# A hybrid attention/mLSTM diffusion layer: attention of all token blocks ahead of the FFN, and the FFN in one pass over split float16 weights

## The chip, the cores and the metric

One core of one Trainium2 chip runs the program. The metric is the device time of one execution in microseconds; the kernel before takes 1610.73 us (median of 3 runs, 1610.1 to 1613.63). The profile shows PE (TensorE; weight loads apart as PEld), DVE (VectorE), ACT (ScalarE), POOL (GpSimd) and the DMA queues, most of which SP issues.

## The reference

One layer over 9 blocks of 128 tokens: block 0 is a prompt that reads itself alone, blocks 1 to 8 are latent tokens that read all latent keys and a cache (9 x 128 keys). All in float32.

```python
h = rmsnorm(x, norm1_w) * (1 + sc1) + sh1
aq, ak, av, mq, mk, mv, mo, mg = split(h @ w_in)            # w_in 1024 x 2832
attn_o = attention(rope(rmsnorm(aq)), keys, vals)           # 8 query heads, 2 key heads, width 64
hm = rmsnorm(mlstm_bidir(mq, mk, mv, gates)) * sigmoid(mo)  # 4 heads, both directions
x  = x + g1 * (concat([attn_o, hm]) @ w_out)                # w_out 1024 x 1024
h2 = rmsnorm(x, norm2_w) * (1 + sc2) + sh2
g, u = split(h2 @ w_gu)                                     # w_gu 1024 x 5632
x  = x + g2 * ((silu(g) * u) @ w_down)                      # w_down 2816 x 1024
y  = rmsnorm(x, final_norm_w)
```

## The kernel before

float32 products are kept by splitting each operand into a high and a low part and adding three products (high by high, high by low, low by high). The input projection and the values product use float16 pairs scaled by powers of two. The output projection and the FFN use pairs of the type fp32r: `load_piece` (L138) loads a weight piece of 512 KB, rounds it on ACT (L151, `whi`) and subtracts on POOL or, every third, on DVE (L134, `wlo`).

**Stages.** Modulation vectors, norm and input projection; four mLSTM heads (`head_project`, `head_mlstm`); then attention, output projection, norm and FFN. These last are done for *chunks* of three blocks (CB = 3, 384 tokens). `GROUPS` and `LAST` (L37, L38) cut the 22 slices of 128 FFN columns (f) into five groups. For each chunk and group, `gate_up` (L1337) makes two products per f with 24 matmuls of 384 columns each (`products`, L1333 to L1335), then tanh on ACT (L1360), two DVE operations (L1361, L1362) and the split of the result into `hl` (L1365 on ACT, L134 on POOL); `down` (L1369) multiplies by w_down with 512-column matmuls (L1152 to L1154) into float32 rows `x1` by `add_gated` (L1138: multiply L1141, add L1142). So all of w_gu and w_down is loaded and split three times, once per chunk.

**Attention.** `attention(c, ...)` (L973) is a generator over the heads of a chunk. A head of a latent block has six 384-column matmuls into the PSUM tile `S` (L1075; one buffer of three banks, so the next head's `S` waits for the exponential), a maximum on DVE (L1077), an exponential on ACT (L1078), two one-column DVE operations (L1079, L1080), the high part of the weights on ACT (L1081), the low part on DVE (L1082), and two DMA transposes that SP issues (L1083, L1084). Two heads later the values product takes 18 matmuls of 256 columns per pair of heads (L999), with ACT (L1001, `ol`) and DVE (L1003, `oT`) behind it. `psum["mm"]` holds four more banks, taken by `bank()`.

**Order.** A scheduler places instructions by priority and its own estimate of time, engine by engine; each engine then runs its list in order. The program order that it starts from is set by hand. Chunk 0's attention (16 heads and the prompt) stands beside the rest of the query projection, `prefill` (L1189, the mLSTM half of the output projection for all blocks) and the first two FFN slices (`gate_up_pair`). Attention of chunks 1 and 2 is woven by `weave` (L62, L1491) into the FFN of the chunk ahead, about one unit of attention for every seven FFN products, and the attention half of the output projection (`attn_out`, L1240) and the second norm (`norm2`, L1285) follow inside that FFN. The last group of the last chunk is `down_last` (L1396), which ends with the final norm block by block.

Of the kernel before, what the change touches and what calls it, by code (L numbers as in the profile page):

```python
# [39 lines left out]
NG = 4  # L40
# [5 lines left out]
def hybrid_step(ctx: ExitStack, tc: tile.TileContext, I: dict, O: dict):  # L46
# [52 lines left out]
    psum = {"mm": ctx.enter_context(tc.tile_pool(name="pB", bufs=4, space=PSUM, reuse_waits="tile"))}  # L99
# [7 lines left out]
    x1_d = [drp.tile([P, D], F32, name=f"x1_d{i}") for i in range(CB)]  # L107
# [50 lines left out]
    def powers(v, n):  # L158

        v = v[0:n]  # L160
        dve.tensor_scalar(out=v[:, 0:1], in0=v[:, 0:1], scalar1=2.0 ** -16, scalar2=None, op0=ALU.max)
# [70 lines left out]
    vsc = cp.tile([P, 4], F32, name="vsc")  # L232

# [14 lines left out]
    one1 = gp.tile([1, P], F32, name="one1")  # L248
    hsc = gp.tile([P, 4], F32, name="hsc")
    hs2 = gp.tile([P, 1], F32, name="hs2")  # L250
    dve.memset(one1, 1.0)

# [126 lines left out]
    dve.memset(G, 0.0)  # L379

# [55 lines left out]
    def ada_rest(adp):  # L436


        def rows_of(n, j, q, half):
            a4 = adp.tile([P, 4, 256], F32, name=nm("a4"), tag="a4", bufs=3)  # L440
# [53 lines left out]
    def evac_kvg(b, ps):  # L494
# [3 lines left out]
        for t in range(2):  # L498
            g4, b4 = (v.rearrange("p (d t h) -> p d t h", d=2, t=2)[:, :, t] for v in (ps[:, 256:272], gbias))
            dve.scalar_tensor_tensor(out=Gv[:, :, t, 4 * b : 4 * b + 4], in0=g4, scalar=kvg.inv, in1=b4, op0=ALU.mult, op1=ALU.add)  # L500

# [261 lines left out]
    def head_mlstm(h, st):  # L763
# [3 lines left out]
        q1 = QT[:, 1, :].rearrange("p (d x) -> p d x", d=2)  # L767
        wvs = {}

        def weighted(b):  # L770
            if b not in wvs:
                wv = wvs[b] = mlp.tile([P, 2, P + 1], F32, name=nm("wv"), tag="wv", bufs=NB)
                dve.tensor_tensor(out=wv, in0=bc(blocks[b][2], 1, [P, 2, P + 1]), in1=bc(q1[:, :, 4 * b + h], 2, [P, 2, P + 1]), op=ALU.mult)
            return wvs[b]
# [9 lines left out]
        weighted(0)  # L784
        for d in range(2):
            weighted(seqs[d][1])
        yield
        for j in range(NBL):
            for d in range(2):
                b = seqs[d][j]  # L790
                pc = bank()
                mm(pc[:, 0 : P + 1], blocks[b][1], wvs[b][:, d], start=True, stop=True)
                if j + 2 < NBL:
                    weighted(seqs[d][j + 2])
# [128 lines left out]
    kwork = k_work(qp, cc, ss, kw)  # L923
    scan = head_mlstm(2, sts[2])
    weave(head_project(3, sts[3]), beside((scan, 1.15), (kwork, 0.5)), 56, 56)
# [8 lines left out]
    mix_spare = [t[:, 2 * (NB + 1) * P :].rearrange("p (k x) -> p k x", k=4) for t in big]  # L934
# [631 lines left out]
```

## Time and profile before

| | |
|---|---|
| median of 3 runs | 1610.73 us |
| the profiled execution | 1617.88 us, span 1616.1 us |
| PE busy | 1521.3 us (94%), 8688 matmul records |
| PEld, DVE, ACT, POOL busy | 1260.8, 940.1, 730.2, 615.8 us |
| mean granted TensorE clock | 0.968 |
| DMA | 227.98 MB, mean 141 GB/s |

A matmul's busy time is its latency, and matmuls overlap; what one adds to PE is the distance from its start to the next one's. Rows of a timeline are: start, duration, engine, line, operation, tiles, shape, count, and in brackets how long the engine was idle before it and who ended that. A windows row is: stretch, length, then busy time and count of PE, PEld, DVE, ACT and POOL, the granted clock, the DMA share and GB/s.

### The profile page before, as it was taken

How to read it: one execution, taken by the hardware profiler on the slowest of the kernel's cores; microseconds unless marked ns; L12 is line 12 of the kernel's file. 1: busy time of each engine (PE TensorE's matmuls, PEld its weight loads, DVE VectorE, ACT ScalarE, POOL GpSimd, SP SyncE). 2: the span in 40 equal slices, each digit the busy share in tenths (PEclk: the TensorE clock that was granted, in tenths of full speed). 3: DMA queues.
4: the chain of work that ended last, by engine and by line, in shares of the span. 5: the costliest groups of instructions: out<-in, count | busy, mean ns of one | idle time of the engine just before them, and what ended most of it. 6: DMA issues, size and time to landing. Idle time of an engine off the chain costs nothing. (4 is left out here: it accounts for less than half of the span.)

```text
span 1616.1 us, 23209 instructions
## 1 busy us (share of the span) xinstructions
PE 1521.3 (94%) x8688; PEld 1260.8 (78%) x8688; DVE 940.1 (58%) x1821; ACT 730.2 (45%) x1240; POOL 615.8 (38%) x376
## 2 busy tenths in 40 slices
PE   5899999899788868999999999999999999999996
PEld 2655665576557758988999999898898989999995
DVE  3944353947787565677753547767764474332445
ACT  3744343435454455655532344565552443333322
POOL 0411020503247453433345344443344445544443
PEclk8899999999899987999999999999999999999998
DMA  9445353211165664787843546787774445534441
GB/s 344 132 131 144 102 134 73 84 19 32 41 171 119 147 159 100 166 194 169 190 146 118 156 144 208 189 180 165 169 178 124 142 134 174 156 122 147 143 130 66
DMA packets 383270, 227.98 MB, mean 141 GB/s; under 512 B 169174, under 2 KB 345766, under 8 KB 383158
## 3 DMA queue, kind: packets, MB, share of 16 engines
q1 hardware_dynamic: 382598, 225.68, 52.9%
q8 instruction: 68, 1.11, 0.3%
q10 hardware_dynamic: 560, 0.83, 0.1%
q14 instruction: 44, 0.36, 0.1%
HBM read 178.80 MB, written 9.33 MB: 116 GB/s over the span
## 5 line engine op out<-in xcount | busy, mean ns | idle before, releaser
L134 POOL TENSOR_TENSOR wlo<-raw,whi 128x1024 fp32r<-128x1024 f32 x146 | 357.8, 2454 | 450.3 <-ACT whi L151 416.4
L151 ACT CAST whi<-raw 128x1024 fp32r<-128x1024 f32 x219 | 224.3, 1025 | 372.0 <-DMA raw<-in_w_gu_dram 127.8
L1334 PE MATMUL mm<-aTl,whi 128*128 128x384 f32 (+2 forms) x1088 | 366.8, 337 | 0.0
L1335 PE MATMUL mm<-aTh,wlo 128*128 128x384 f32 (+2 forms) x1088 | 366.4, 337 | 0.0
L1333 PE MATMUL mm<-aTh,whi 128*128 128x384 f32 (+2 forms) x1088 | 365.1, 337 | 0.9 <-DVE tn L1361 0.9
L1333 PEld LDWEIGHTS mm<-aTh,whi 128*128 128x128 f32 x1088 | 206.9, 190 | 2.1 <-DVE tn L1361 1.5
L1334 PEld LDWEIGHTS mm<-aTl,whi 128*128 128x128 f32 x1088 | 206.9, 190 | 1.0 <-POOL aTl L134 0.3
L1335 PEld LDWEIGHTS mm<-aTh,wlo 128*128 128x128 f32 x1088 | 207.0, 190 | 0.1
L134 DVE TENSOR_TENSOR wlo<-raw,whi 128x1024 fp32r<-128x1024 f32 (+1 forms) x73 | 88.2, 1208 | 132.9 <-ACT whi L151 132.7
L1152 PE MATMUL mm<-whi,hl 128*128 128x512 f32 x372 | 147.0, 398 | 1.0 <-ACT hl L1365 0.9
L1153 PE MATMUL mm<-wlo,hl 128*128 128x512 f32 x372 | 147.2, 397 | 0.0
L1154 PE MATMUL mm<-whi,hl 128*128 128x512 f32 x372 | 144.4, 397 | 0.7 <-POOL hl L134 0.7
L1082 DVE SCALAR_TENSOR_TENSOR pl<-pr,st,ph 128x1152 f16<-128x1152 f32 x64 | 109.5, 1711 | 46.7 <-ACT ph L1081 46.6
L487 PE MATMUL wi<-ipair,hT 128*128 128x384 f16 (+2 forms) x384 | 124.9, 326 | 2.8 <-ACT ipair L215 2.8
L488 PE MATMUL wi<-ipair,hT 128*128 128x384 f16 (+2 forms) x384 | 124.9, 325 | 0.0
L489 PE MATMUL wi<-ipair,hT 128*128 128x384 f16 (+2 forms) x384 | 124.4, 325 | 0.3 <-POOL hT L134 0.3
L1361 DVE SCALAR_TENSOR_TENSOR tn<-tn,mm 128x384 f32<-128x384 f32 (+2 forms) x68 | 36.7, 540 | 144.4 <-PE mm L1335 110.0
L134 POOL TENSOR_TENSOR hl<-tn,hl 128x384 fp32r<-128x384 f32 x66 | 81.9, 1241 | 96.5 <-ACT hl L1365 90.4
L1142 DVE TENSOR_TENSOR x<-x,t 128x512 f32<-128x512 f32 x102 | 116.1, 1158 | 0.8
L1078 ACT ACTIVATE pr<-S,st 128x1152 f32<-128x1152 f32 x64 | 78.3, 1223 | 80.4 <-DVE st L1077 77.6
L1141 DVE TENSOR_TENSOR t<-mm,gl 128x512 f32<-128x512 f32 x106 | 70.8, 683 | 40.6 <-PE mm L1154 15.8
L1077 DVE TENSOR_REDUCE st<-S 128x1 f32<-128x1152 f32 x64 | 86.5, 1351 | 13.2 <-PE S L1075 12.8
(370 smaller groups left out, 2678.0 us busy)
## 6 DMA issues: line engine op xcount, KB each, us to landing
raw<-in_w_gu_dram SPq DMA_DIRECT2D x132, 512.0 KB
raw<-in_w_down_dram SPq DMA_DIRECT2D x60, 512.0 KB
a<-in_w_ada_dram SPq DMA_DIRECT2D x32, 512.0 KB
gl<-g_d SPq DMA_DIRECT2D x36, 256.0 KB
aw<-in_w_ada_dram SPq DMA_DIRECT2D x16, 512.0 KB
iraw<-in_w_in_dram SPq DMA_DIRECT2D x32, 256.0 KB
raw<-in_w_out_dram SPq DMA_DIRECT2D x15, 512.0 KB
x<-in_x_sample_dram SPq DMA_DIRECT2D x13, 512.0 KB
```

Of the source, the lines that this page charges most:

```text
L134: (dve if eng == "dve" else pool).tensor_tensor(out=out, in0=full, in1=hi, op=ALU.subtract)
L151: nc.scalar.copy(hi[:, :n], raw[:, :n])
L487: mm(ps[:, :n], ah, wh[:, k % 2, c0 : c0 + n], start=(k == 0), stop=False)
L488: mm(ps[:, :n], ah, wl[:, k % 2, c0 : c0 + n], start=False, stop=False)
L489: mm(ps[:, :n], al, wh[:, k % 2, c0 : c0 + n], start=False, stop=(k == KD - 1))
L1142: eng.tensor_tensor(out=x1[:, cs], in0=x1[:, cs], in1=t, op=ALU.add)
L1152: mm(ps, ah, wh[:, k % 2, :], start=(k == 0), stop=False)
L1153: mm(ps, ah, wl[:, k % 2, :], start=False, stop=False)
L1154: mm(ps, al, wh[:, k % 2, :], start=False, stop=(k == nk - 1))
L1333: mm(ps, wh[:, k, :], th[:, k, :], start=(k == 0), stop=False)
L1334: mm(ps, wh[:, k, :], tl[:, k, :], start=False, stop=False)
L1335: mm(ps, wl[:, k, :], th[:, k, :], start=False, stop=(k == KD - 1))
```

## The change

Attention, `prefill`, the attention half of the output projection (`out_rest`) and `norm2` run for all nine blocks before the FFN. `FILL` is the amount of other matmul work, in us by the writer's unit costs, that the program order puts beside one head. x1 and the normed h2 of all blocks stay in SBUF, h2 as float16 pairs scaled by one power of two (`bound_h2`). The FFN then makes one pass: four groups of 6, 6, 6 and 4 slices; each w_gu piece is loaded once, measured (ACT, sum of squares), scaled and split into float16 (`Piece`); w_down is split once into float16 pairs and written to a DRAM tensor `wd_d` (`split_down`), from which `down9` loads ready pairs, three times in all. A group's results wait as float32 (`tn`), and `rescale` makes float16 pairs of them under one scale for the group while the next group's products run. At the end of attention its PSUM tiles are released and the FFN gets eight banks. No POOL work is left in the FFN. The mLSTM scan's weighting is done per direction, and some tiles move between pools.

```diff
-GROUPS = [(0, 4), (4, 4), (8, 4), (12, 5), (17, 5)]
-LAST = [(0, 5), (5, 5), (10, 4), (14, 4), (18, 4)]
+GROUPS = [(0, 6), (6, 6), (12, 6), (18, 4)]
+SLOTS = 24
+FILL = 2.2
...
+    def out_rest():
+        ws = out_pieces(0)
+        for b in range(NB):
+            while b not in done:
                 yield False
...
+            for n in range(2):
                 ps = out_block(ws, n, th, tl)
+                add_gated(x1[b], ps, gx[n] if b == 0 else gs[n], n, pool)
+                yield 2.8
+            if b > 0:
+                yield from norm2(b - 1)
+            rs[b] = stats(x1[b : b + 1])[0]
+            yield 0.1
...
+    fill = chain(prefill(), out_rest())
+    for v in att:
+        due = min(due + v, 5.0)
+        while due > 0.0:
+            u = next(fill, None)
+            if not u:
+                break
+            due -= u
+    emit(fill)
...
+    pieces[0].load()
+    pieces[0].measure()
+    pieces[0].scales()
+    pieces[0].convert()
+    es_at.close()
+    es_p.close()
+    es_b.close()
+    bp = ctx.enter_context(tc.tile_pool(name="bp", bufs=1, reuse_waits="tile"))
+    psum["mm"] = ctx.enter_context(tc.tile_pool(name="p8", bufs=8, space=PSUM, reuse_waits="tile"))
...
+    def gate_up9(g):
...
+                products(ps[:, 0:CT], wh, wl, h2[c][:, 0], h2[c][:, 1])
...
+            tn = bp.tile([P, CT], F32, name=nm("tn"), tag="hl", bufs=SLOTS)
+            act(tn, pg[:, 0:CT], AF.Tanh, scale=p.v[:, 6:7])
+            dve.scalar_tensor_tensor(out=tn, in0=tn, scalar=1.0, in1=pu[:, 0:CT], op0=ALU.add, op1=ALU.mult)
+            dve.scalar_tensor_tensor(out=tn, in0=tn, scalar=p.v[:, 7:8], in1=pg[:, 0:CT], op0=ALU.mult, op1=ALU.mult)
+            act(jk[:, 0:CT], tn, AF.Abs, accum_out=g["st"][:, i : i + 1])
...
+    def down9(g):
+        for c in range(NCH):
+            for n in range(2):
+                banks = [bank() for _ in range(CB)]
+                for j in range(0, g["nf"], 2):
+                    w = down_piece(g, j, n)
+                    for i, ps in enumerate(banks):
+                        down_products(ps, g, j, b, w)
```

**Where instructions move.** First PE during the attention of chunk 1. Before (S is a head's scores, `mm` with `aTh`/`aTl` the FFN's gate and up product, `po` the values product):

```order
L1333 MATMUL mm_10156<-aTh_9420,whi_10159 128x384
L1334 MATMUL mm_10156<-aTl_9421,whi_10159 128x384
L1335 MATMUL mm_10156<-aTh_9420,wlo_10160 128x384
L1333 MATMUL mm_10156<-aTh_9420,whi_10159 128x384
L1334 MATMUL mm_10156<-aTl_9421,whi_10159 128x384
L1075 MATMUL S_10135<-kst_4226,qT_9905 128x384 x6
L999 LDWEIGHTS vs
L999 MATMUL po_10189<-phT_9996,vs 128x256
L1335 MATMUL mm_10156<-aTh_9420,wlo_10160 128x384
L1333 MATMUL mm_10156<-aTh_9420,whi_10159 128x384
```

In the changed kernel, late in attention:

```order
L1029 LDWEIGHTS vs
L1029 MATMUL po_7528<-plT_7308,vs 128x256
L1103 MATMUL S_7465<-kst_4270,qT_7084 128x384 x6
L1103 MATMUL S_7557<-kst_4271,qT_7084 128x384 x6
L1103 MATMUL S_7602<-kst_4271,qT_7084 128x384 x6
L1029 LDWEIGHTS vs
L1029 MATMUL po_7622<-phT_7423,vs 128x256
L1029 LDWEIGHTS vs
L1029 MATMUL po_7622<-plT_7424,vs 128x256
```

Before, FFN matmuls stand on both sides of a head's scores; now the scores of three heads follow each other with nothing between.

Next DVE at the same place. Before (one head; t and x are `add_gated`):

```order
L1077 TENSOR_REDUCE st_11429<-S_11430 128x1
L1141 TENSOR_TENSOR t_2146_11303<-mm_11269,gl_11255 128x512
L1079 RECIPROCAL st_11429<-st_11429 128x1
L1142 TENSOR_TENSOR x_1020_5218<-x_1020_5218,t_2146_11303 128x512
L1080 TENSOR_SCALAR st_11429<-st_11429 128x1
L1141 TENSOR_TENSOR t_2154_11351<-mm_11306,gl_11255 128x512
L1141 TENSOR_TENSOR t_2155_11354<-mm_11307,gl_11255 128x512
L1142 TENSOR_TENSOR x_1020_5218<-x_1020_5218,t_2154_11351 128x512
L1142 TENSOR_TENSOR x_1020_5218<-x_1020_5218,t_2155_11354 128x512
L1082 SCALAR_TENSOR_TENSOR pl_11428<-pr_11426,st_11429,ph_11427 128x1152
```

In the changed kernel (three heads):

```order
L1105 TENSOR_REDUCE st_7650<-S_7651 128x1
L1110 SCALAR_TENSOR_TENSOR pl_7600<-pr_7598,st_7601,ph_7599 128x1152
L1107 RECIPROCAL st_7650<-st_7650 128x1
L1108 TENSOR_SCALAR st_7650<-st_7650 128x1
L1105 TENSOR_REDUCE st_7729<-S_7730 128x1
L1110 SCALAR_TENSOR_TENSOR pl_7649<-pr_7647,st_7650,ph_7648 128x1152
L1107 RECIPROCAL st_7729<-st_7729 128x1
L1108 TENSOR_SCALAR st_7729<-st_7729 128x1
L1110 SCALAR_TENSOR_TENSOR pl_7728<-pr_7726,st_7729,ph_7727 128x1152
L1033 SCALAR_TENSOR_TENSOR oT_7527<-po_7761,vsc,ol_7780 64x128 x2
L1105 TENSOR_REDUCE st_7789<-S_7790 128x1
```

The FFN's operations are gone from between a head's; the low part `pl` of a head stands behind the next head's maximum in the first two and ahead of it in the third.

Last, PE where attention ends. Before, chunk 2's output projection (`mx`) runs straight into FFN products that were ready:

```order
L1184 MATMUL mm_12270<-whi_12180,mx_12251 128x512
L1185 MATMUL mm_12270<-wlo_12181,mx_12251 128x512
L1186 MATMUL mm_12270<-whi_12180,mx_12251 128x512
L1333 MATMUL mm_12309<-aTh_9420,whi_12312 128x384
L1334 MATMUL mm_12309<-aTl_9421,whi_12312 128x384
L1335 MATMUL mm_12309<-aTh_9420,wlo_12313 128x384
```

In the changed kernel:

```order
L1183 MATMUL mm_8285<-wlo_6822,kst_4270 128x512
L1184 MATMUL mm_8285<-whi_6821,kst_4271 128x512
L1362 MATMUL mm_8356<-fv_8351,ones 128x2
L1285 LDWEIGHTS wpair_8366
L1285 MATMUL mm_8400<-h_1399_7094,wpair_8366 128x384
L1286 LDWEIGHTS wpair_8366
L1286 MATMUL mm_8400<-h_1399_7094,wpair_8366 128x384
```

Behind the last output block stands the 2-column matmul that measures the first FFN weight piece (L1362), and only behind it the first FFN product, whose weights (`wpair`) are converted by that measure.

More of the change, by code (lines that the diff above doesn't have):

```diff
@@ L1160, in out_pieces @@
-    def out_pieces(half, own=None):
+    def out_pieces(half):
         ws = []
@@ L1166, in out_pieces @@
                 rows = w_out[r0 : r0 + 2 * P, n * 512 : (n + 1) * 512].rearrange("(a p) n -> p a n", p=P)
[L1167 to L1168 removed]
+                pieces.append(load_piece([(full_view, rows)], (2, 512), 1))
             ws.append(pieces)
         return ws
[L1172 to L1178 removed]
     def out_block(ws, n, th, tl):
@@ L1277, in stats @@
+            yield 0.1
     def stats(rows):
@@ new lines, in hybrid_step @@
+    pieces = [Piece(0, lambda: wp.tile([P, 1024], F32, name=nm("braw"), tag="raw", bufs=2), ("whi", "wlo"))]
+    pieces += [Piece(f) for f in range(1, NF)]
+    pieces[0].load()
[7 more added lines that the diff above has]
+    psum["mm"] = ctx.enter_context(tc.tile_pool(name="p8", bufs=8, space=PSUM, reuse_waits="tile"))
+    pieces[1].load()
```

716 lines of the change are left out of this document (370 added, 346 removed).

## The prediction

> **What bounds the kernel now.** I read the busy time by stage first, because the share over the whole span (PE 94%) is a mean over unlike stages.
>
> ```profile
> span 1616.1 us, 23209 instructions
> PEclk8899999999899987999999999999999999999998
> 0.00:445.00 445.00, 398.80 (x2614) 253.73 (x2615) 253.22 (x779) 199.52 (x521) 92.20 (x107) 0.94 0.40 112
> 445.00:600.00 155.00, 134.88 (x664) 102.00 (x662) 111.22 (x189) 78.57 (x107) 85.61 (x52) 0.92 0.67 155
> 600.00:650.00 50.00, 39.73 (x231) 36.66 (x230) 24.45 (x55) 25.96 (x44) 16.56 (x10) 0.80 0.41 90
> 650.00:1616.00 966.00, 947.92 (x5185) 868.39 (x5183) 551.17 (x801) 426.19 (x570) 421.47 (x207) 1.00 0.58 155
> ```
>
> The reader is to see four stages. Up to 445 us nothing of weight is changed. From 445 to 650 us, chunk 0's attention, PE is idle for about 30 us and its clock falls to 0.92 and 0.80. From 650 us, the FFN with the attention of chunks 1 and 2 inside, PE is idle for 18 of 966 us at full clock: PE bounds this stage, and DVE (57%), ACT and POOL have room. So the weights split three times cost nothing there; the FFN's price is its matmuls, and attention's long DVE and ACT chain is covered by them.
>
> The price of a matmul is the distance between starts. From timelines of PE, the first and last row of four unbroken runs (40, 12, 29 and 33 rows of one shape):
>
> ```profile
> 843.10 0.34 PE L1335 MATMUL mm<-aTh,wlo 128*128 128x384 f32 x1
> 849.86 0.34 PE L1335 MATMUL mm<-aTh,wlo 128*128 128x384 f32 x1
> 169.49 0.33 PE L487 MATMUL wi<-ipair,hT 128*128 128x384 f16 x1
> 171.28 0.33 PE L489 MATMUL wi<-ipair,hT 128*128 128x384 f16 x1
> 515.60 0.40 PE L1185 MATMUL mm<-wlo,aTh 128*128 128x512 f32 x1
> 522.14 0.39 PE L1186 MATMUL mm<-whi,aTl 128*128 128x512 f32 x1
> 443.21 0.39 PE L487 MATMUL mm<-ipair,hT 128*128 128x512 f16 x1
> 450.13 0.38 PE L489 MATMUL mm<-ipair,hT 128*128 128x512 f16 x1
> ```
>
> That is 6.76/39 = 0.173 us for fp32r of 384 columns, 1.79/11 = 0.163 for float16 of 384, 6.54/28 = 0.234 for fp32r of 512, 6.92/32 = 0.216 for float16 of 512.
>
> **The FFN.** By the code it has 22 x 2 x 3 x 24 = 3168 products of 384 columns and 22 x 9 x 2 x 3 = 1188 of 512, before and after. By the pitches they take 3168 x 0.173 + 1188 x 0.234 = 826 us before and 516 + 257 = 773 us after: 53 us saved. This is the whole gain on PE. Removed besides are two thirds of the w_gu loads and splits, and all POOL work; these lay beside PE and are worth nothing by themselves. New work beside PE: per slice f and three chunks, DVE has six operations on `tn`, two piece splits, one w_down split and three pair splits; even at the 1.4 us that a 1152-column operation takes below, the four large ones and nine small ones stay under 15 us, against 144 x 0.163 + 54 x 0.216 = 35 us of PE. The round trip of w_down pairs through DRAM has over 100 us before the first group needs it, and each 512 KB piece then serves 18 matmuls (3.9 us), five buffers deep. I cost both at nothing; uncovered they would cost a few us at a group's start. For the group scales and the first pieces' waits I add 5: the FFN takes 778 us.
>
> The Trainium skill ("TensorE: Matmul & The Clock Gate", section "Back-to-back issue gap") gives about 131 ns as the sustained spacing of 512-column matmuls beside an isolated 216; this trace's unbroken run has 0.216. By 131 ns the 1188 matmuls would take 101 us less than by the row; the row stands.
>
> **Attention now stands almost alone.** What it costs is the loop of one head, since S has one buffer: scores on PE, maximum on DVE, exponential on ACT, next scores. Timelines of two places of chunk 0, a filled one (522) and one where PE had nothing else (574 to 589):
>
> ```profile
> 522.36 1.21 PE L1075 MATMUL S<-kst,qT 128*128 128x384 f32 x6
> 523.61 1.36 DVE L1077 TENSOR_REDUCE st<-S 128x1 f32<-128x1152 f32 x1 [0.29 <-PE S L1075]
> 525.01 1.22 ACT L1078 ACTIVATE pr<-S,st 128x1152 f32<-128x1152 f32 x1 [0.37 <-DVE st L1077]
> 526.24 0.28 PE L999 MATMUL po<-plT,vs 128*128 128x256 f16 x1 [2.12 <-DMA plT<-pl]
> ...
> 574.65 1.34 DVE L1077 TENSOR_REDUCE st<-S 128x1 f32<-128x1152 f32 x1
> 576.27 1.21 ACT L1078 ACTIVATE pr<-S,st 128x1152 f32<-128x1152 f32 x1
> 577.63 2.29 PE L1075 MATMUL S<-kst,qT 128*128 128x384 f32 x6 [1.19 <-ACT pr L1078]
> 579.95 0.42 PE L999 MATMUL po<-phT,vs 128*128 128x256 f16 x1
> 579.96 1.36 DVE L1077 TENSOR_REDUCE st<-S 128x1 f32<-128x1152 f32 x1 [0.90 <-PE S L1075]
> 583.15 0.35 PE L999 MATMUL po<-plT,vs 128*128 128x256 f16 x1
> 588.32 1.35 DVE L1077 TENSOR_REDUCE st<-S 128x1 f32<-128x1152 f32 x1
> ```
>
> At full clock a loop is 1.25 (scores to maximum) + 1.40 + 1.22 + 0.15 (exponential's end at 577.48 to the next scores at 577.63) = 4.0 us. Where PE has idled, the same six score matmuls take 2.29 instead of 1.21, and sixteen values matmuls from 579.95 to 583.15 stand 0.213 us apart: the clock is halved and the loop is 5.1. The interval measured there, 574.65 to 579.96, is 5.3. The rows of the other operations:
>
> ```profile
> L1077 DVE TENSOR_REDUCE st<-S x64: 1342/1350/1359, 451.9 to 1197.6; 128x1 f32<-128x1152 f32 x64
> L1082 DVE SCALAR_TENSOR_TENSOR pl<-pr,st,ph 128x1152 f16<-128x1152 f32 x64 | 109.5, 1711 | 46.7 <-ACT ph L1081 46.6
> L1081 ACT ACTIVATE ph<-pr,st 128x1152 f16<-128x1152 f32 x64 | 80.5, 1258 | 22.7 <-issue 8.3 <-ACT pr L1078 8.0 <-DVE st L1080 4.2
> ```
>
> In the changed order `pl` stands ahead of the next maximum for about half the heads. There DVE must first wait for `ph` (1.26 us after about 0.6 for the sum and two one-column operations) and then do `pl` (1.4 undisturbed, 1.71 on average): the maximum comes 3.3 us after the exponential instead of 1.4 to 2.5, and the loop is about 5.9. Between 4.0, 5.1 and 5.9, and beside the measured 5.3, I take 5.2 us.
>
> How many heads have nothing to fill them? Counting PE rows of the changed order between the scores of successive heads, 20 of 63 intervals hold more than 5 us of matmuls by the pitches, together 145 us; the other 43 hold less, mostly the scores and half a values product (1.0 to 3.0 us). The rest of the query projection sits beside the first two, the mLSTM half of the output projection beside heads 12 to 30, and the last 30 heads have one output block per eight. So attention is 145 + 20 x 0.5 (a share of waits like the 2.12 us at 526.24) + 43 x 5.2 = 379 us from the first head's maximum (451.9, taken unchanged) to the last one's. PE's own work there is 248 us. Before, 48 of the 64 heads cost PE only their matmuls. The two DMA transposes of a head stay as they were.
>
> **From the last head to the FFN** nothing covers the chain any more. The last head before, by rows of DVE and SP, and the groups of what follows:
>
> ```profile
> 1197.55 1.35 DVE L1077 TENSOR_REDUCE st<-S 128x1 f32<-128x1152 f32 x1
> 1203.51 1.30 SPq L1084 DMA_TRANSPOSE plT<-pl  x1
> 1211.26 0.70 DVE L1003 SCALAR_TENSOR_TENSOR oT<-po,vsc,ol 64x128 f32<-64x128 f32 x2 [4.83 <-ACT ol L1001]
> L134 POOL TENSOR_TENSOR kst<-oT,kst 128x512 fp32r<-128x512 f32 x3 | 3.8, 1262 | 2.6 <-ACT kst L1256 2.6
> L1142 POOL TENSOR_TENSOR x<-x,t 128x512 f32<-128x512 f32 x18 | 28.5, 1587 | 8.9 <-DVE t L1141 6.6 <-DVE ry L130 1.8 <-DVE rv L124 0.5
> L1281 ACT ACTIVATE jk<-x 128x1024 bf16<-128x1024 f32 x15 | 15.8, 1052 | 9.7 <-DVE x L1142 7.0 <-POOL x L1142 2.6
> L130 DVE SCALAR_TENSOR_TENSOR ry<-rt,ry 128x1 f32<-128x1 f32 x27 | 5.9, 225 | 0.5
> L151 ACT CAST whi<-raw 128x1024 fp32r<-128x1024 f32 x207 | 216.9, 1049 | 344.2 <-DMA raw<-in_w_gu_dram 127.8 <-DMA raw<-in_w_down_dram 54.3 <-PE mm L1334 53.5
> ```
>
> Maximum to the end of `oT` is 14.4 us. Then the split of `oT` on POOL (1.3 and its cast) and 24 matmuls of 0.234: 7 us. The first weight piece's scales stand on DVE behind the last block's norm: two adds on POOL (3), the sum of squares (1.05), 12 and 8 small operations of 0.2 (4), one cast (1.05), handovers: 10. Together 31 us until the first FFN product, against a seam before that was filled by ready products.
>
> **The end.** Last matmul and last operation before:
>
> ```profile
> 1602.84 0.40 PE L1420 MATMUL mm<-whi,hl 128*128 128x512 f32 x1
> 1611.60 0.75 DVE L1431 SCALAR_TENSOR_TENSOR x<-x,ry,fw 128x512 f32<-128x512 f32 x1
> ```
>
> 13.3 us to the span's end. Now nine blocks end this way instead of three, each with about 6 us of DVE work against 24 x 0.216 = 5.2 us of PE; I add 4, so 17.
>
> **Sum**, as a span: 451.9 + 379 + 31 + 778 + 17 = 1657 us, against 1616.1. The profiled execution took 1617.88, 1.8 more than its span, and the median of the runs is 7.15 below that: 1657 + 1.8 - 7.15 = 1651 us.
>
> **The rivals.**
>
> *The heads run at full clock and faster follows.* With 4.0 us for the 43 unfilled heads attention is 145 + 10 + 172 = 327, and the whole 1600 us. For it: the loop from 522 to 526 is that short where the clock is full. Against it: the halved clock at 577 came after gaps of about 2 and 1 us, and half the heads have `pl` in the loop. The point from which it decides is (1616.1 - 17 - 778 - 31 - 451.9 - 155) / 43 = 4.3 us per unfilled head. The Trainium skill (the same page, section "HAM oscillation — how this bites in real kernels") says the clock falls only after PE gaps over about 3.4 us. By that rule gaps of 4.0 - 1.2 = 2.8 us would keep full clock and this rival would hold; this trace had the half clock after shorter gaps.
>
> *The heads are as slow as the two measured ones.* From 574.65 to 588.32 two unfilled heads took 6.8 us each, other work in DVE's and ACT's queues among it. Then attention is 155 + 292 = 447 and the time 1719. Against it: in the changed order that other work is rarer.
>
> *Gain and loss cancel*: 4.3 us per unfilled head, 1611 us.
>
> *The float16 FFN does better than its pitch*, as by the 131 ns above: 1651 - 101 = 1550. No row supports it.
>
> **How the numbers follow.** Forecast (1618 to 1690 as its own range, from 4.4 to 6.1 us a head): 0.57. Full clock: 0.23. Slow heads: 0.13. Cancelled: 0.06. Better pitch: 0.01. A change within 0.2% (1607.5 to 1614) is about what cannot be told from none. Faster 0.24, same 0.06, slower 0.70. The range 1592 to 1705 takes in most of the full-clock case and a part of the slow heads.
>
> **What would show it.** FFN pitches of 0.163 and 0.216 and some 778 us from its first product to the last; first maximum near 452 us; last maximum near 830, with intervals of 5 to 6 us and a PEclk of 0.6 to 0.9 over the last 30 heads; 25 to 35 us from the last maximum to the first FFN product. The forecast is wrong if unfilled heads take under 4.3 us, or if FFN products wait for weights.

## The result, and the profile after

The changed kernel takes 1704.96 us (median as recorded) against 1612.18 before: 1.0566 times as long, 95% interval 1.0543 to 1.0589. It is slower, as forecast, but by 5.7% instead of 2.5%: 1704.96 lies inside the edge of the range (1592 to 1705) by 0.04 us, which is chance, and outside the forecast's own (1618 to 1690). One execution of it, the profiled one, took 6463 us with products of 512 columns 0.84 us apart, a disturbance that no other run showed (the others lie between 1701.16 and 1705.86); the median as recorded counts it, the ratio leaves it out, and everything below is read from a second profile of the same kernel.

> The changed kernel itself, run again for an undisturbed profile; nothing is edited. Forecast's steps: first per-head maximum near 452 us, last near 830 (intervals of 5 to 6 us where PE has no other work), 25 to 35 us from the last maximum to the first FFN product, 778 us of FFN, 17 us from the last matmul to the end: span 1657. Measured was about 47 us more. If the unfilled heads are as slow as the two measured before (6.8 us), the last maximum stands near 890 and the FFN at 778. If the FFN waits for weights or runs at a lower clock, the last maximum stands near 830 and the FFN takes about 825.

It took 1704.21 us, 1.9 more than its span. From the page, and from a windows view whose edges are the first head's maximum, the last head's maximum, the first FFN product and the last matmul:

```profile
span 1702.3 us, 22914 instructions
PEclk8999999999879997776769999999999999999998
0.00:437.40 437.40, 397.24 (x2658) 253.20 (x2659) 268.15 (x840) 201.12 (x524) 91.55 (x107) 0.97 0.42 119
437.40:858.40 421.00, 314.13 (x1525) 243.09 (x1522) 304.55 (x535) 240.96 (x341) 116.61 (x77) 0.82 0.56 110
858.40:894.70 36.30, 13.16 (x52) 9.68 (x52) 11.67 (x43) 17.23 (x30) 6.05 (x5) 0.66 0.46 136
894.70:1684.30 789.60, 782.62 (x4418) 434.15 (x4418) 340.96 (x790) 256.56 (x488) 11.92 (x9) 0.99 0.31 96
1684.30:1702.30 18.00, 0.33 (x2) 0.00 (x0) 13.26 (x46) 5.34 (x12) 2.52 (x2) 0.64 0.32 117
```

The five lengths are the five terms of the forecast's sum:

| | forecast | measured | difference |
|---|---|---|---|
| start to first maximum | 451.9 | 437.4 | -14.5 |
| first to last maximum | 379 | 421.0 | +42 |
| last maximum to first FFN product | 31 | 36.3 | +5.3 |
| FFN, first to last product | 778 | 789.6 | +11.6 |
| last matmul to end | 17 | 18.0 | +1 |
| span | 1657 | 1702.3 | +45 |

So the question is attention: 421 us for 314 us of busy PE (by the pitches 248), 305 of DVE and 241 of ACT. No engine is full, and the granted clock is 0.82. The maxima, the scores and the two groups of values products, then what PE waited for in attention:

```profile
L1105 DVE TENSOR_REDUCE st<-S x64: 1341/1357/1359, 437.4 to 858.4; 128x1 f32<-128x1152 f32 x64
PE S L1103 <- ACT pr L1106: 49.0, 21, 3.9
PE po L1029 <- DMA phT<-ph: 20.4, 8, 4.4
PE po L1029 <- DMA plT<-pl: 16.1, 14, 2.6
```

Two pieces of its timeline. The first is the plain loop of a head without other work; the second a head whose scores stand behind a values product:

```profile
782.17 2.29 PE L1103 MATMUL S<-kst,qT 128*128 128x384 f32 x6 [2.79 <-ACT pr L1106]
784.50 1.36 DVE L1105 TENSOR_REDUCE st<-S 128x1 f32<-128x1152 f32 x1 [0.94 <-PE S L1103]
785.89 1.22 ACT L1106 ACTIVATE pr<-S,st 128x1152 f32<-128x1152 f32 x1 [1.32 <-DVE st L1105]
787.25 2.29 PE L1103 MATMUL S<-kst,qT 128*128 128x384 f32 x6 [2.79 <-ACT pr L1106]
...
797.08 1.41 DVE L1110 SCALAR_TENSOR_TENSOR pl<-pr,st,ph 128x1152 f16<-128x1152 f32 x1
798.52 1.30 SPq L1112 DMA_TRANSPOSE plT<-pl  x1
798.57 2.29 PE L1103 MATMUL S<-kst,qT 128*128 128x384 f32 x6 [2.80 <-ACT pr L1106]
...
800.89 1.36 DVE L1105 TENSOR_REDUCE st<-S 128x1 f32<-128x1152 f32 x1 [1.99 <-PE S L1103]
802.28 1.22 ACT L1106 ACTIVATE pr<-S,st 128x1152 f32<-128x1152 f32 x1 [2.05 <-DVE st L1105]
...
803.65 0.40 PE L1029 MATMUL po<-plT,vs 128*128 128x256 f16 x1 [2.56 <-DMA plT<-pl]
...
807.04 0.42 PE L1029 MATMUL po<-plT,vs 128*128 128x256 f16 x1
807.11 2.02 PE L1103 MATMUL S<-kst,qT 128*128 128x384 f32 x6
...
809.17 1.36 DVE L1105 TENSOR_REDUCE st<-S 128x1 f32<-128x1152 f32 x1 [0.47 <-PE S L1103]
```

The plain loop takes 5.08 us, 787.25 less 782.17, because the scores run at half clock (2.29 us; 1.21 at full). In the second piece the exponential is done at 803.50, and S is free. But in PE's order the next scores stand behind seventeen matmuls of a values product that had been waiting 2.6 us for the transpose of `pl`, issued at 798.52. They run at half clock, 0.213 us apart, until 807.04, and so the scores begin 3.6 us late. The maximum at 809.17 comes 8.3 us after the one at 800.89.

This can be added up over all 63 intervals. From each exponential's end to the next one's there are six pieces: until the scores begin, the scores, until the maximum begins, the maximum, until the exponential begins, the exponential. Summed, with "filled" for intervals in which, from maximum to maximum, more than 5 us of matmuls by the pitches start (the scores' own 1.04 us included):

| us | count | scores late (PE) | scores | maximum late (DVE) | maximum | exponential late (ACT) | exponential | sum |
|---|---|---|---|---|---|---|---|---|
| filled | 18 | 65.1 | 22.7 | 16.5 | 24.3 | 1.2 | 22.0 | 152 |
| with a values product | 24 | 38.7 | 36.7 | 11.8 | 32.6 | 4.9 | 29.3 | 154 |
| scores alone | 21 | 4.6 | 43.2 | 9.8 | 28.5 | 3.5 | 25.7 | 115 |
| all | 63 | 108.4 | 102.6 | 38.0 | 85.3 | 9.8 | 76.9 | 421 |

At the bare 4.0 us the 45 unfilled intervals would take 180 us; they take 269, 6.0 each. By the shortest of each piece (0.14, 1.21, 0.04, 0.03) the 89 us above are: scores late on PE 37, half clock on scores 25, DVE 20, ACT 7. Of the 37, about 27 are values products, nearly all after PE had waited for a transpose, and 10 are fill in three intervals that hold less than 5 us of it. Most of those values products run at half clock (0.213 us a matmul; at 483.76, at full clock, 0.11), so the clock's share is more than the 25.

The FFN, the only place with a gain, from two unbroken runs of 84 and 40 rows:

```profile
1132.01 0.38 PE L1502 MATMUL mm<-wd,hl 128*128 128x512 f16 x1
1149.93 0.38 PE L1504 MATMUL mm<-wd,hl 128*128 128x512 f16 x1
1194.77 0.33 PE L1286 MATMUL mm<-h,wpair 128*128 128x384 f16 x1
1201.11 0.33 PE L1286 MATMUL mm<-h,wpair 128*128 128x384 f16 x1
PE mm L1362 <- ACT jk L1357: 6.7, 4, 4.3
```

17.92/83 = 0.216 and 6.34/39 = 0.163 us, the forecast's pitches. The last line, of the waits in the FFN, is nearly all that PE lost there to weights: the scale of a piece four times stood behind ACT's measure of it.

### The profile page after: what moved, and what is told of

Read it like the earlier page. It is cut to its first block, busy times and chain, and to the rows that moved or that the text cites. A ratio compares the mean times of both kernels' runs of the same rounds, so it can differ in the third digit from the quotient of the medians.

```text
span 6461.6 us, 22914 instructions
## 1 busy us (share of the span) xinstructions
PE 6364.4 (98%) x8651; PEld 2721.2 (42%) x8651; DVE 915.9 (14%) x2250; ACT 732.5 (11%) x1392; POOL 219.5 (3%) x200
## 5 line engine op out<-in xcount | busy, mean ns | idle before, releaser
L1286 PE MATMUL mm<-h,wpair 128*128 128x384 f16 x1056 | 956.8, 906 | 0.0
L1285 PE MATMUL mm<-h,wpair 128*128 128x384 f16 x1056 | 950.0, 900 | 6.8 <-ACT wpair L1379 6.8
L1287 PE MATMUL mm<-h,wpair 128*128 128x384 f16 x1056 | 954.0, 904 | 0.0
L500 PE MATMUL wi<-ipair,hT 128*128 128x384 f16 (+2 forms) x384 | 514.1, 1339 | 0.0
L501 PE MATMUL wi<-ipair,hT 128*128 128x384 f16 (+2 forms) x384 | 513.6, 1339 | 0.0
L499 PE MATMUL wi<-ipair,hT 128*128 128x384 f16 (+2 forms) x384 | 507.5, 1322 | 2.9 <-ACT ipair L216 2.9
L1503 PE MATMUL mm<-wd,hl 128*128 128x512 f16 x396 | 437.0, 1104 | 0.0
L1502 PE MATMUL mm<-wd,hl 128*128 128x512 f16 x396 | 436.7, 1104 | 0.0
L1504 PE MATMUL mm<-wd,hl 128*128 128x512 f16 x396 | 436.3, 1104 | 0.0
L1285 PEld LDWEIGHTS <-wpair 128*128 128x128 f16 x1056 | 237.8, 225 | 412.2 <-issue 404.3
L1287 PEld LDWEIGHTS <-wpair 128*128 128x128 f16 x1056 | 236.5, 224 | 409.0 <-issue 408.9
L1286 PEld LDWEIGHTS <-wpair 128*128 128x128 f16 x1056 | 235.8, 223 | 400.9 <-issue 400.9
L1103 PE MATMUL S<-kst,qT 128*128 128x384 f32 x384 | 333.4, 1125 | 39.0 <-ACT pr L1106 39.0
L1103 PEld LDWEIGHTS S<-kst,qT 128*128 128x128 f32 x384 | 233.4, 633 | 107.1 <-ACT pr L1106 56.5
L499 PEld LDWEIGHTS <-hT 128*128 128x128 f16 x432 | 134.3, 311 | 303.5 <-issue 303.3
L1029 PE MATMUL po<-phT,vs 128*128 128x256 f16 x292 | 239.9, 822 | 15.3 <-DMA phT<-ph 13.9
L500 PEld LDWEIGHTS <-hT 128*128 128x128 f16 x432 | 136.9, 317 | 257.3 <-issue 257.2
L1029 PE MATMUL po<-plT,vs 128*128 128x256 f16 x292 | 241.9, 828 | 3.0 <-DMA plT<-pl 2.9
L501 PEld LDWEIGHTS <-hT 128*128 128x128 f16 x432 | 135.8, 314 | 258.3 <-issue 258.3
L1029 PEld LDWEIGHTS <-vs 128*128 128x128 f16 x584 | 143.7, 259 | 188.9 <-issue 171.5
```

The lines of the kernel that those rows point to most:

```text
L499: mm(ps[:, :n], ah, wh[:, k % 2, c0 : c0 + n], start=(k == 0), stop=False)
L500: mm(ps[:, :n], ah, wl[:, k % 2, c0 : c0 + n], start=False, stop=False)
L501: mm(ps[:, :n], al, wh[:, k % 2, c0 : c0 + n], start=False, stop=(k == KD - 1))
L1029: mm(po[:, 0:256], v, rhs(t, n), start=(n == 0 and t == 0), stop=(n == nk - 1 and t == 1))
L1103: mm(S[:, n, 0:CT], qT[:, h, :], kst[kv][:, t, n * CT : (n + 1) * CT], start=(t == 0), stop=(t == 1))
L1285: mm(ps, wh[:, k, :], th[:, k, :], start=(k == 0), stop=False)
```

## The experiments

Two theories at first. **Clock**: an unfilled head is slow because PE idles and is halved. **Queue**: scores wait in PE's order behind values products and fill, and maxima behind `pl`. A third came from them: **loop**, S has one buffer, so every lateness on PE, DVE or ACT is added into one chain. All kernels are the changed one with the edit shown. Single runs of the changed kernel differ by up to 5 us, so stages are compared, not only times.

**Filling the gaps with idle matmuls.**

```diff
-    psum mm: bufs=4
+    psum mm: bufs=3; a bank W of its own
+        wps = psum["W"].tile(...)          # e1: eight of these per head
+        mm(wps, vs[...], ph_of_the_head_before[:, 0:512])
+        # e10: one of a single column that reads st[:, 0:1], the head's own maximum, then five on vs
```

> The changed kernel with eight float16 matmuls of 512 columns added per head from the second block on; they write a PSUM bank of their own that nobody reads, and take the head before's `ph` as moving operand, so that they fall into the gap between two heads' scores. (The other PSUM ring has three banks instead of four.) CLOCK theory, an unfilled head is slow because PE idles and its clock is halved (scores 2.29 instead of 1.21 us, a values product 3.4 to 3.8 instead of 1.9): the scores-only loop falls from 5.1 to 4.0 to 4.3, heads with values from 6.4 to about 5, attention from 421 to about 365, the span to 1640 to 1655, and the granted clock in attention goes to 0.95 or more. QUEUE theory, heads are late because scores stand on PE behind a values product that waits for its DMA transpose, and a maximum on DVE behind the low part: the extra 1.7 us per head on PE cost or do nothing; span 1700 to 1725 whatever the clock.

> One S buffer, the changed kernel with five added float16 matmuls of 512 columns per head that start when the head's maximum is done (the first reads `st`) and so fill the time of the exponential (1.22 us, five take 1.08); unlike in the first experiment they don't wait for `ph` of the head before and should not hold up the scores. The shared PSUM ring has three banks, which cost 30 us ahead of the first maximum in the first experiment and will here. CLOCK theory: scores summed over the heads fall from 103 to about 80 us, values products shorten too, and nothing else grows: attention 375 to 395. QUEUE theory: the time that the clock gives back goes into waits for transposes, `pl` and fill: attention 405 to 425. Span: attention plus about 1310.

Of both the maxima, of e1 two rows of scores and three rows of the waits, of e10 one row of the waits:

```profile
L1106 DVE TENSOR_REDUCE st<-S x64: 1339/1357/1359, 467.4 to 907.1; 128x1 f32<-128x1152 f32 x64
804.16 1.31 PE L1104 MATMUL S<-kst,qT 128*128 128x384 f32 x6 [2.70 <-ACT pr L1107]
808.27 1.31 PE L1104 MATMUL S<-kst,qT 128*128 128x384 f32 x6 [0.50 <-ACT pr L1107]
PE po L1029 <- DMA plT<-pl: 14.2, 12, 2.2
PE po L1029 <- DMA phT<-ph: 5.8, 7, 1.6
PE wps L1111 <- ACT ph L1115: 11.7, 13, 3.8
```

```profile
L1106 DVE TENSOR_REDUCE st<-S x64: 1340/1357/1359, 466.9 to 903.5; 128x1 f32<-128x1152 f32 x64
PE wps L1110 <- DVE st L1106: 36.7, 20, 6.1
```

The clock came back (scores summed over the heads 84 and 89 us instead of 103; loops of 4.11, 808.27 less 804.16), and attention grew, to 439.7 and 436.6, more than either theory allowed. More than the scores gave back went into scores late on PE (129 and 139 us instead of 108) and, in the first, into late maxima (54 instead of 38). In e1 the values products wait for the transpose of `pl` as before (14 us for 16) and less for that of `ph` (6 for 20), but the added matmuls wait too, 12 and 37 us, take time themselves, and hold what stands behind them; and attention's other products have three banks instead of four here. So this is no clean price of the clock: the full clock did not shorten the stage in these kernels, and what it would give without the added matmuls is not shown. The three banks cost 30 us ahead of the first maximum, which is the rest of the 1754.5 and 1748.9 us.

**Spreading the fill.** `FILL` paces only the order in which the program is written; the scheduler places a half-block as soon as it can run. Here each waits for a head:

```diff
+    now = 0 * st_of_latest_head + 1        # one column, on DVE
-    nc.scalar.copy(th, psv)                # once per block
+    act(th, psv, AF.Copy, scale=now)       # once per half-block
-    fill = chain(prefill(), out_rest())
+    fill = chain(prefill(0, 5), out_rest(0, 4), prefill(5, NB), out_rest(4, NB))
```

(`FILL` is 1.9 here, and the query projection is written earlier, at unit costs of 0.4 for 1.4; the latter also in all kernels with two S buffers.)

> The same work, but the mLSTM half of the output projection is kept back: each of its 18 half-blocks waits for a column of the latest head before it (its first copy is scaled by 0*x+1 of that head's `st`), and it runs in the order blocks 0-4, then the attention half for 0-3, then blocks 5-8, then the attention half for 4-8 (w_out pieces are loaded four times instead of twice). So most heads get one half-block of 2.8 us instead of 18 heads getting two and 30 nearly none. PLACEMENT theory, an unfilled head leaves some 3 us of PE idle and a half-block there is free and keeps the clock up: the 18 filled heads fall from 8.4 to about 6 and the others do not rise; attention 330 to 375, span 1620 to 1660. CHAIN theory, the loop of maximum, exponential, low part and transposes sets the pace whatever PE does: attention stays within 410 to 430, span 1695 to 1715.

> Both edits together, with four added matmuls per head instead of eight. If CLOCK and PLACEMENT are both right: attention near 320 to 350, span 1605 to 1640, below each alone. If only the clock matters, as the first; if only the placement, as the second, plus up to 20 us for the added matmuls.

```profile
L1106 DVE TENSOR_REDUCE st<-S x64: 1341/1357/1359, 441.1 to 846.2; 128x1 f32<-128x1152 f32 x64
```

405.1 us, 16 less, and 1691.2 in all: a small gain, just below what the chain theory allows and far from the 46 to 91 us of the placement theory. Eighteen intervals were still filled, at 8.2 us each. With four idle matmuls besides, 416.4 and 1732.2 us, 30 of them again ahead of attention: no gain from the two together, but the placement's result and 11 us more, the last case of that expectation.

**Leaving out the low part of the weights.**

```diff
-    dve.scalar_tensor_tensor(out=pl, ...)
-    dma_t(plT[...], pl...)
-    for t in range(2): mm(po, v, rhs(t, n), ...)
+    for t in range(1): mm(po, v, rhs(t, n), ...)
```

> One buffer of S again, everything else as changed, but the low part of the attention weights is left out: no `pl` on DVE, no transpose of it, and 9 instead of 18 matmuls in a values product. (The output is then a less exact attention.) In the changed kernel's trace the 45 unfilled heads take 89 us more than the bare 4.0 us each: 37 are scores behind a values product on PE, 25 the halved clock on scores, 20 maxima behind `pl` and other DVE work, 7 ACT. QUEUE theory (values products waiting for a transpose, and `pl`, hold up the one chain): some 27 of the 37 and most of the 20 go, and some of the filled heads' DVE waits; attention 355 to 380, span 1635 to 1662. CLOCK theory (PE idles, so it is slow): PE idles even more, the scores stay at 2.29 us in more heads; attention 400 to 425, span 1680 to 1705.

```profile
L1105 DVE TENSOR_REDUCE st<-S x64: 1344/1357/1359, 438.2 to 837.6; 128x1 f32<-128x1152 f32 x64
PE po L1029 <- DMA phT<-ph: 34.2, 11, 4.1
```

399.4 us, 22 less (1678.2 in all, where part of the gain is the shorter chain behind the last head). Late maxima fell from 38 to 10 us and late scores from 108 to 99, but PE now idled more and the scores rose from 103 to 114. So the two theories are coupled: of the 38 us that the queues gave back on DVE and PE, 11 were lost to the clock and 5 to later exponentials. And the late scores hardly fell, because the values products now wait for the transpose of `ph`, 34.2 us where it was 20.4 and another 16.1 for `pl`: taking one of the two transposes away left the wait nearly whole, although the DMA engines were 0.33 busy instead of 0.56. The result lies at the lower edge of the clock theory's 400 to 425, for a reason that neither theory had.

**`ol` on DVE.** Whether ACT's copy of one values product delays the next head's `ph`, and so its transposes:

```diff
-    act(ol, po[64:128, 0:256], AF.Copy, scale=vsc[64:128, 1:2])
+    dve.tensor_scalar(out=ol, in0=po[64:128, 0:256], scalar1=vsc[64:128, 1:2], scalar2=None, op0=ALU.mult)
```

> The changed kernel with one S buffer; only `ol`, the scaled copy of half a values product, moves from ACT to DVE. In the changed kernel ACT waits 35 us in all for values products before `ol`, and the next head's `ph` stands behind it; the transposes and the next values product follow `ph`. If that order is what makes values products late: scores behind PE work fall by 15 to 30 us, attention 390 to 408. If not (DVE takes over the wait, the transposes take their time anyway): attention 412 to 430.

Attention 416.8, the whole 1703.1. Late scores fell by 20 us, as expected of the first alternative, but late maxima rose by 15: the wait moved to DVE. One queue's wait taken away reappears in another.

**Two buffers for S.** This takes away the chain itself:

```diff
-    for name, bufs in (("po", 1), ("S", 1)):     # beside four banks mm
+    for name, bufs in (("po", 1), ("S", 2)):     # beside one bank mm
```

(The query projection goes block by block, the mLSTM half of blocks 7 and 8 singly, and `norm2` takes its two banks one after the other, since there is only one.)

> S gets two buffers (six PSUM banks); in return attention's other products (query projection, output projection, norm transposes) share one bank instead of four, with the query projection taken block by block. Nothing else is edited. From the changed kernel's trace: of the 421 us from first to last maximum, 252 are 63 times the bare loop of 4.0 us (scores, maximum, exponential), 99 are scores that stand on PE behind other matmuls (fill, and values products waiting for a DMA transpose), 26 the halved clock on scores, 35 maxima behind other DVE work, 8 exponentials behind other ACT work. LOOP theory: these add up only because the next scores must wait for the exponential to free S; with two buffers a head's scores run during the exponential before it and the stage goes to what DVE has to do (306 us busy in the stage): attention 315 to 360, span 1595 to 1645. TRANSPOSE theory: the values products' waits for DMA transposes stop PE anyway: attention 400 to 425, span 1680 to 1710. One bank for the fill could cost some of either.

> Two S buffers as in the run before, together with the paced order of the output projection of the second experiment (which alone gave 405 us of attention and a span of 1689). LOOP theory: attention 310 to 345, span 1590 to 1630. TRANSPOSE theory: attention near 400, span 1680 to 1700.

Attention 406.1 us and 1696.9 in all (paced: 405.1, but 81.5 more until the first FFN product, 1726.7). By the number this is the transpose theory's case. But 56 of the 63 intervals took 3.8 us on average, as the loop theory says, and seven took 12 to 54 us; five of these stand at block boundaries, where the transposes that turn the next block's queries waited for their turn at the one bank. Turning them in a slot of S:

```diff
-            ps = bank()
+            ps = psum["S"].tile([P, 3, 512], F32, name=nm("S"), tag="S")[:, 0, :]
```

> As the run with two S buffers, but the four transposes that turn a block's queries use a slot of S instead of the one shared bank. In that run 56 of the 63 intervals took 3.8 us on average, and seven at block boundaries 12 to 54 us, where the turning stood in the bank's order behind output projection that was not ready. LOOP theory: those seven go, attention 315 to 350, span 1595 to 1645. TRANSPOSE theory (values products wait for DMA transposes whatever S does): the boundaries stay above 20 us each, attention 395 to 415.

> The same with the paced order of the output projection. LOOP theory: attention 310 to 340, span 1590 to 1630; within 10 us of the run before, since with two S buffers it matters less where the fill stands. TRANSPOSE theory: attention 395 to 415.

The groups of maxima and of FFN products of the first (e6), and two successive maxima on DVE:

```profile
L1108 DVE TENSOR_REDUCE st<-S x64: 1335/1352/1359, 439.1 to 812.8; 128x1 f32<-128x1152 f32 x64
L1289 PE MATMUL mm<-h,wpair x1056: 322/326/528, 860.1 to 1582.3; 128*128 128x384 f16 x176
601.52 1.36 DVE L1108 TENSOR_REDUCE st<-S 128x1 f32<-128x1152 f32 x1 [0.30 <-PE S L1106]
679.86 1.36 DVE L1108 TENSOR_REDUCE st<-S 128x1 f32<-128x1152 f32 x1 [0.41 <-PE S L1106]
```

Attention 373.7 us, 47 less, in 1672.9, between the ranges of the two theories; without the one interval of 78 us the mean is 4.8 us a head, filled ones included, against 6.7. The 78 us stand where e4 already had 37: the heads now outrun the fill. By the code `oT` has three buffers, and the products that read the oldest are written behind all half-blocks of the other half, ten of which, and four of its own, ran in this interval. Paced, attention is 345.8, but the fill held back ran after the last head, the stretch to the first FFN product is 109.6 us, and the whole is 1707.2, not within 10 us of e6 as expected. Writing the output projection in portions, so that `oT` is read in time:

```diff
+    fill = chain(prefill(0, 3), out_rest(0, 2), prefill(3, 6), out_rest(2, 4), prefill(6, 9), out_rest(4, 9))  # e9
+    pieces.append(load_piece([(full_view, rows)], (2, 512), 1000))    # e9: w_out's low parts on POOL
+    fill = chain(prefill(0, 5), out_rest(0, 4), prefill(5, 9), out_rest(4, 9))    # e11, e12
+    norm_rope(...): every second query block on DVE instead of POOL               # e11, e12
+    es_p.close(); psum["mm"] = pool p8 of eight banks; emit(fill)                 # e12
```

> Two S buffers with the turning on S, and the output projection written in six portions (mLSTM half of blocks 0-2, attention half of 0-1, mLSTM half of 3-5, attention half of 2-3, and the rest), so that `oT` (three buffers) is consumed in time; w_out's low parts on POOL. In the run with two S and its own turn slot one interval was 78 us: a values product waited for an `oT` buffer that was to be read by output projection standing behind 14 half-blocks of the mLSTM half. If that wait is what is left of attention's cost: no interval over 30 us, attention 300 to 335; twelve half-blocks (34 us) then follow the last head, so the span comes to 1625 to 1655. If the stall only moves: span 1665 to 1690.

> The likeliest best of the two-S kernels: output projection in four portions (mLSTM half of blocks 0-4, attention half of 0-3, and the rest), not held back, and the rotation of every second query block on DVE instead of POOL so that the output projection can begin earlier. If fill that is ready in time is what lacked: no interval over 35 us, attention 325 to 350, ten half-blocks (28 us) behind the last head, span 1630 to 1660, still 1.3 to 3 per cent over the kernel before. If the work only moves behind the last head: attention 330 to 350 and 90 us or more from the last maximum to the first FFN product, span 1670 to 1700.

> The run before (two S buffers, output projection in four portions), but S, `po` and the one bank are released, and the eight FFN banks opened, ahead of the rest of the output projection instead of behind it. BANK theory (one bank makes each half-block wait for its eviction): the stretch from the last maximum to the first FFN product falls from 93 to 55 to 65 us, span 1635 to 1645. CHAIN theory (the rest waits for the last heads' `oT`, splits and norms): it stays within 80 to 93 us, span 1658 to 1672.

Windows of e9 and of e11, attention and from the last maximum to the first FFN product, and the two groups of e12:

```profile
443.60:778.60 335.00, 259.57 (x1351) 201.48 (x1350) 284.23 (x482) 226.36 (x307) 136.41 (x80) 0.87 0.76 154
778.60:887.00 108.40, 63.19 (x240) 45.41 (x240) 46.84 (x129) 46.55 (x82) 39.36 (x29) 0.75 0.29 75
```

```profile
440.80:772.40 331.60, 260.89 (x1388) 203.40 (x1386) 282.30 (x512) 220.92 (x302) 77.09 (x52) 0.91 0.73 146
772.40:865.20 92.80, 51.29 (x205) 36.99 (x206) 44.85 (x128) 44.76 (x80) 32.32 (x24) 0.74 0.31 79
```

```profile
L1110 DVE TENSOR_REDUCE st<-S x64: 1305/1350/1359, 440.3 to 772.8; 128x1 f32<-128x1152 f32 x64
L1292 PE MATMUL mm<-h,wpair x1056: 322/326/528, 864.8 to 1583.7; 128*128 128x384 f16 x176
```

Attention fell to 335 and 332 us, DVE now 85% busy in it, which is what the loop theory said of two buffers, and the longest interval to 20 and 33 us, which bears out the wait for `oT`. But the stage as a whole, from the first maximum to the first FFN product, tells how much was kept:

| | first maximum | attention | to first FFN product | both | time, us |
|---|---|---|---|---|---|
| changed kernel | 437.4 | 421.0 | 36.3 | 457.3 | 1704.2 |
| e2 paced | 441.1 | 405.1 | 36.2 | 441.3 | 1691.2 |
| e8 no low part | 438.2 | 399.4 | 33.5 | 432.9 | 1678.2 |
| e4 two S | 433.9 | 406.1 | 48.9 | 455.0 | 1696.9 |
| e6 two S, own turn | 439.1 | 373.7 | 47.3 | 421.0 | 1672.9 |
| e9 in six portions | 443.6 | 335.0 | 108.4 | 443.4 | 1697.7 |
| e11 in four portions | 440.8 | 331.6 | 92.8 | 424.4 | 1670.8 |
| e12 banks before the rest | 440.3 | 332.5 | 92.0 | 424.5 | 1673.5 |

Behind the first FFN product every kernel takes 804 to 811 us. Of the 89 us that e11 saves in attention 33 are kept: ten half-blocks (28 us of products) are left behind the last head, and there the chain of split, output projection, add, norm and transposes of one block after the other is bare again. e12 shows that the one bank is not why: with eight the stretch is as long. So the work moved behind the last head, as the second alternative of e11 said for the stretch (90 us or more), while the span, 1669.2, is just below its 1670 to 1700. e9's, 1695.9, is above both of its alternatives. e11 is 1.0372 times the kernel before (1.0355 to 1.0389), e12 1.0369 (1.034 to 1.0397): with e6's single run the best of these, and still slower than before. No kernel was found that beats it.

Not tried: taking a values product a pair of heads later, with a third buffer for the turned weights, so that PE would not stand waiting for its transposes.

## Why the prediction was right and wrong

**The bound and the sign: right.** The FFN's gain is only the pitch of its matmuls. The measured pitches are 0.163 and 0.216 us, and 3168 and 1188 of them make the 773 us of the forecast. The gain of 53 us stays a product of pitches, since the FFN before has no stretch of its own to compare; it and the loss in attention are of the expected kind, and the loss is the larger.

**The FFN: right to 1.5%.** 789.6 instead of 778. Weights were not waited for except for the 6.7 us at the scale of a piece; the 44 matmuls of those scales and the last block's transposes, which the sum had not listed, lie in the rest.

**131 ns: fell.** By the Trainium skill's "TensorE: Matmul & The Clock Gate", section "Back-to-back issue gap", the products of 512 columns would have stood 131 ns apart; the run of 84 shows 216 ns.

**The unfilled head: the step that failed.** "Between 4.0, 5.1 and 5.9, and beside the measured 5.3, I take 5.2 us", for 43 heads, 224 us. Counted from scores to scores, as the forecast counted, there are again 20 filled intervals and 43 unfilled, and the 43 take 6.0 each, 259 us: 35 of the 54 us of the miss. (By the table above, from maximum to maximum, it is 45 at 6.0, 269 us.) The 20 take 163 us instead of 155. The choice of 5.2 let one delay act at a time: the half clock (5.1) or `pl` ahead of the maximum (5.9). The trace has both, and a third that the step did not have: scores behind values products that had waited for a transpose, about 27 of the 89 us above the bare loop.

The 6.0 lies within the 4.4 to 6.1 from which the forecast made its own range; by itself it gives 1686 us. The other 19 us are small terms that the range held fixed: filled intervals 8, the way to the FFN 5, the FFN 12, the end 1, span to median 8, less 14.5 at the first maximum.

The rival built on the two heads of the old trace, 1719, came nearer than the forecast (by 14 us; the forecast missed by 54), but not for what its two heads showed. In both of them the scores began 0.15 us after the exponential, with no values product in the way. The first, 5.3 us, is mostly the half clock; in the second, 8.4 us, the maximum at 588.32 came 3.4 us after the scores' end, on DVE behind small operations and `pl`. From the timelines of the kernel before, in the second:

```profile
582.27 1.21 ACT L1078 ACTIVATE pr<-S,st 128x1152 f32<-128x1152 f32 x1
583.63 1.31 PE L1075 MATMUL S<-kst,qT 128*128 128x384 f32 x6
586.98 1.42 DVE L1082 SCALAR_TENSOR_TENSOR pl<-pr,st,ph 128x1152 f16<-128x1152 f32 x1
```

So it is in part luck that this rival came nearer.

**Why no single cause gives it back.** One buffer of S makes one chain of PE, DVE and ACT, and each of the three has other work in its queue. Raising the clock, spreading the fill, moving `ol`, leaving out the low part: each reduced its own piece and let another grow. Attention changed by +19 and +16, -16, -4 and -22 us, where the theories had promised at least 26, 46, 13 and 41 less. Cutting the chain (two buffers) gave only 15 us while the turning stood at the one bank, and 47 to 89 us in attention after that; with the stretch behind the last head, to which part of the work moved, 36 us are left in e6, 33 in e11 and e12, 14 in e9 and 2 in the paced one. That much of the loss is shown to hang on the one buffer, together with what these kernels changed beside it; how the 6.0 us divide between clock, transposes and `pl` is an account from the trace, which these runs do not separate.

**The half clock: right, and the rule for it wrong here.** Scores at 2.29 us follow gaps of 2.79 us, and the clock of 0.75 over the last 30 heads (670 to 858 us) lies within the 0.6 to 0.9 expected. The Trainium skill (the same page, section "HAM oscillation — how this bites in real kernels") has the clock fall after gaps over about 3.4 us; by this the plain loop at 782.17, with its gaps of 2.79 us, would have kept full clock and taken 4.0 us, and it took 5.08 at a granted clock of 0.50. In the first experiment scores stayed at 1.31 us, at a granted clock of 1.00, right after a gap of 2.70 us, where PE was busier before it; before the change they took 2.29 after a gap of 1.19. So in these rows it is not the length of the last gap alone that decides.

**From the last head to the FFN, and the end: right.** 36.3 for 31, 18.0 for 17.

**The first maximum: 14.5 us too late in the forecast.** It was carried over "unchanged". The mLSTM scan does its weighting per direction in the changed kernel, and in windows of 50 us PE's granted clock from 250 to 350 us is 1.00 instead of 0.93. Which edit does it was not tested. It hid a third of the miss in attention.

**From span to median: 8 us.** The forecast took 7.15 us off because before's profiled execution was that much above its median. The changed kernel's was 0.75 below its median (1704.21, 1704.96). With 45 us of span these 8 make the 54 us of the miss. An offset of one execution belongs to that execution.

## What to carry to other kernels

When work that was woven into a matmul-bound stage is moved out to stand alone, price it as a chain: list every engine's queue between two steps of the loop, and add the delays, since with one buffer between the engines they do not overlap. Where a trace shows such a loop even twice, read from its rows what made each turn long, and ask of every delay whether the new order keeps it, before setting the measured period aside. And before doubling the buffer that closes the loop, ask what the freed engines will overrun next and what will be left to do after the last iteration: here 89 us came out of attention and 33 out of the kernel.

## What the hardware showed unexpectedly

The clock was halved for scores between gaps of 2.8 us (2.29 us for six matmuls that take 1.21) and stayed full after a gap of 2.70 us where idle matmuls kept PE busier. A DMA transpose of 128 x 1152 float16 issued at 798.52 released its reader at 803.65: 5.1 us, more than a whole head of the bare loop (4.0 us); in the stage with 64 pairs of them the DMA engines were 0.56 busy at 110 GB/s. With half of the transposes left out they were 0.33 busy, and PE still waited 34.2 us for the other half.
